# The down projection of a transformer block as seven block products instead of eight

## The chip, the cores and the metric

The kernel runs on one core of one Trainium2 chip. The metric is the device time of one execution in microseconds (us), lower being better. A difference under 0.2% (about 2.8 us here) can't be told from no change.

## The reference

One block of a hybrid model on a sequence of 1024 rows with 1024 features, in float32: normalisation and input projection, a sparse attention and a gated linear attention side by side, an output projection with residual, and a feed-forward part. Only the last part matters here:

```python
h = h + jnp.concatenate([o_nsa, o_gla], axis=-1) @ w_out[l]
u = causal_dwconv(rms_norm(h, ffn_norm[l]) @ w_up[l], conv_w[l], conv_b[l])
gate, up = jnp.split(u, 2, axis=-1)
h = h + (jax.nn.silu(gate) * up) @ w_down[l]
```

The product in the last line is the down product: activations of 1024 rows by 2816 channels times weights of 2816 channels by 1024 features. Its result is added to `h` and leaves the chip.

## The kernel before, in words

Every matrix product is made of float32r factors in two parts. ScalarE copies a float32 tile into a "high" part (`hi_of`, L57), VectorE subtracts that from the source and keeps the rest as the "low" part (`lo_of`, L60); together that is a `split` (L89). TensorE then makes three matmuls for each pair of tiles, high by high, high by low and low by high. Each is 128x128 by 128x512 and adds into one PSUM bank of 128x512.

The kernel is recorded with a tile framework that has a scheduler of its own: it puts the instructions of each engine in an order, and each engine then works strictly in that order. SyncE (SP) issues nearly all loads, one after another; a load whose buffer is still in use holds up all loads behind it. Buffers come from pools on two ends of the memory; a pool that opens where an older one was closed has to wait for that one's last readers, tile by tile.

The work runs in stages: input projection and attention (to about 600 us), output projection (to about 730 us), up product (to 1157 us), down product (to the end).

The up product runs over 22 channel blocks `j`. Its blocks from the fourth on are already made as one level of Strassen's scheme: `up` (L834) makes seven products `prod` of 12 matmuls, in the order B11, T2, T1, T3, B21, B22, T4 of its right-hand factors (`fac`, split tiles that stay in memory for the whole stage). The `gated` step (L771) applies the convolution and the gate with ScalarE and VectorE and writes 128 channels by 1024 rows to a scratch tensor `act_d` in DRAM.

The down product (L869 to L912) runs over two halves of the features (`hf`) and, in each, over eight row tiles of 128 rows. `act_load` brings the activations of one row tile back in three loads and splits them with all 22 channel blocks in one tile; the weights `wD` of a half are loaded and split once, and stay. Each row tile takes 22 x 3 = 66 matmuls into one bank; VectorE adds `h` (L911) and ScalarE's queue sends the tile out (L912). That is 2 x 8 x 66 = 1056 matmuls. A row tile needs all 22 channel blocks, so its last loads wait for the last block of the up product.

Of the kernel before, what the change touches and what calls it, by code (L numbers as in the profile page):

```python
# [34 lines left out]
def body(tc, I, out, tap=lambda name, ap: None):  # L35
# [51 lines left out]
    act_d = [dr.tile([NT, 128, 8, 128], F, name=f"act_d{i}") for i in range(3)]  # L87
# [567 lines left out]
    k2 = pool(es, "k2", 18, side="right")  # L655
# [6 lines left out]
    for f in ("B11", "B21", "B22", "B12"):  # L662
        facp[f] = pool(sF, "fac" + f, side="right")
        fac[f] = tuple(facp[f].tile([128, 4, 512], R, name=f"f{f}{p}", tag=p) for p in "hl")
    h = {(t, hf): k2_tile(name="h") for t in range(NT) for hf in range(2)}
    facp["T3"] = pool(sF, "facT3", side="right")
# [63 lines left out]
    with ExitStack() as sp:  # L730
        fc = pool(sp, "fc")
        cw = fc.tile([128, 2 * NJ, 3], F, name="cw")
        cb = fc.tile([128, 2 * NJ], F, name="cb")
        SY.dma_start(cw, I["cw"])
        SY.dma_start(cb, I["cb"])
        for f in ("T3", "T1", "T2"):
            if f not in facp:
                facp[f] = pool(sF, "fac" + f, side="right")
            fac[f] = tuple(facp[f].tile([128, 4, 512], R, name=f"f{f}{p}", tag=p) for p in "hl")
        wr = pool(sp, "wr", 3)  # L740
        wsp = pool(sp, "wsp", 1)
        ttp = pool(sp, "ttp", 4)
# [28 lines left out]
        def gated(j, us):  # L771
            ys = []
            for b in range(2):
# [9 lines left out]
            SY.dma_start(act_d[j // 8][:, :, j % 8].rearrange("t p q -> p t q"),  # L783
                         ys[1].rearrange("p (t q) -> p t q", q=128))
# [81 lines left out]
    sF.close()  # L866


    with ExitStack() as sp:  # L869
        pad = pool(sp, "pad")  # L870
        pad.tile([128, 192], F, name="pad")
        dB = pool(sp, "dB", 32, side="right")
        dA = pool(sp, "dA", 20, side="right")
        ar = pool(sp, "ar", 2)
        ah_a = pool(sp, "ah_a", 4)
        ah_p = pool(sp, "ah_p", 10)
        pd = pool(sp, "pd", 4, PSUM)

        def act_load(t):
            got = []  # L880
            for i in range(3):
                n = min(8, NJ - 8 * i)
                raw = ar.tile([128, 8, 128], F, name="araw")[:, :n]
                SY.dma_start(raw, act_d[i][t, :, :n])
                x, y = ((ah_p if i else ah_a).tile([128, 8, 128], R, name=m, tag="ahl")[:, :n] for m in ("ah", "al"))
                split(x, y, raw, V)
                got += [(x[:, j], y[:, j]) for j in range(n)]
            return got

        for hf in range(2):  # L890
            sl = slice(hf * 512, hf * 512 + 512)
            dws = {}
            for ts in ([0, 1], [2], [3], [4], [5], [6], [7]):
                acts = {t: act_load(t) for t in ts}
                ps = {t: pd.tile([128, 512], F, name="pd") for t in ts}
                for j in range(NJ):
                    if j not in dws:
                        raw = k2_tile(name="wdraw")
                        SY.dma_start(raw, I["wD"][j, :, sl])
                        dws[j] = tuple((dA if j < 10 else dB).tile([128, 512], R, name=n, tag="d") for n in ("dh", "dl"))  # L900
# [115 lines left out]
```

## Time and profile before

| | |
|---|---|
| median of 3 runs | 1418.25 us (1416.62 to 1418.8) |
| profiled execution | 1420.06 us, of which its span is 1418.3 us |
| granted TensorE clock, mean over the span | 0.983 of full speed |
| TensorE (PE) busy | 1349.2 us, 95% |
| VectorE (DVE) busy | 1003.6 us, 71% |
| ScalarE (ACT) busy | 688.3 us, 49% |
| GpSimd (POOL) busy | 334.6 us, 24%, nothing after the output projection |
| DMA | 174.19 MB, mean 123 GB/s |

PE is the row of matmuls and PEld that of the weight loads, which overlap them. A matmul row lasts 0.39 us, but one starts every 0.227 us, so that the distance of starts, not the row's length, is its price. The same holds on VectorE and ScalarE, whose successive instructions overlap by about 0.1 us. In square brackets at a row's end stands how long the engine was idle before it and what ended that.

### The profile page before, as it was taken

How to read it: one execution, taken by the hardware profiler on the slowest of the kernel's cores; microseconds unless marked ns; L12 is line 12 of the kernel's file. 1: busy time of each engine (PE TensorE's matmuls, PEld its weight loads, DVE VectorE, ACT ScalarE, POOL GpSimd, SP SyncE). 2: the span in 40 equal slices, each digit the busy share in tenths (PEclk: the TensorE clock that was granted, in tenths of full speed). 3: DMA queues.
4: the chain of work that ended last, by engine and by line, in shares of the span. 5: the costliest groups of instructions: out<-in, count | busy, mean ns of one | idle time of the engine just before them, and what ended most of it. 6: DMA issues, size and time to landing. Idle time of an engine off the chain costs nothing.

```text
span 1418.3 us, 19798 instructions
## 1 busy us (share of the span) xinstructions
PE 1349.2 (95%) x6750; PEld 1125.3 (79%) x6750; DVE 1003.6 (71%) x2433; ACT 688.3 (49%) x1390; POOL 334.6 (24%) x491
## 2 busy tenths in 40 slices
PE   6998989999999999999969999999999989999998
PEld 5876878887888887777858888888888867887887
DVE  7985856878787789843889888888788884325320
ACT  5332656777665677653544544444444462214210
POOL 5343655538444464425200000000000000000000
PEclk9999999999999999999989999999999998999999
DMA  8536673325221332116630222222222165437430
GB/s 306 179 126 231 186 239 111 110 70 161 85 93 57 102 103 79 38 53 195 194 127 15 89 76 88 70 79 89 90 89 76 58 215 182 163 134 245 159 126 23
DMA packets 92904, 174.19 MB, mean 123 GB/s; under 512 B 9970, under 2 KB 44675, under 8 KB 92803
## 3 DMA queue, kind: packets, MB, share of 16 engines
q1 hardware_dynamic: 66818, 108.95, 23.7%
q0 software_dynamic: 10368, 37.75, 8.8%
q10 hardware_dynamic: 15616, 26.22, 5.1%
q8 instruction: 53, 0.87, 0.3%
q14 instruction: 49, 0.39, 0.1%
HBM read 130.95 MB, written 41.94 MB: 122 GB/s over the span
## 4 chain that ended last, share of the span: by engine, by line
PE 78%; DVE 10%; DMA 4%; ACT 3%; issue 2%; POOL 2%; SPq 0%; ACTq 0%; DVEq 0%; POOLq 0%
PE pd L906 16%; PE O L466 4%; PE z L118 4%; PE z L120 4%; PE z L119 4%; PE S L448 4%; PE pt L459 3%; PE uX L764 3%; PE uX L766 3%; PE uX L765 3%; PE uZ L764 3%; PE uZ L766 3%; PE uZ L765 3%; PE uW L764 3%; PE uW L766 3%; PE uW L765 3%
## 5 line engine op out<-in xcount | busy, mean ns | idle before, releaser
L118 PE MATMUL z<-whi,xt 128*128 128x512 f32 (+1 forms) x384 | 143.1, 373 | 5.7 <-DVE vv L204 2.7
L906 PE MATMUL pd<-dh,ah 128*128 128x512 f32 x352 | 137.7, 394 | 7.4 <-ACT ah L57 4.7
L906 PE MATMUL pd<-dh,al 128*128 128x512 f32 x352 | 138.6, 394 | 4.7 <-DVE al L60 4.7
L119 PE MATMUL z<-wlo,xt 128*128 128x512 f32 (+1 forms) x384 | 141.1, 367 | 0.4 <-DMA w<-in_w_dram 0.4
L120 PE MATMUL z<-whi,xt 128*128 128x512 f32 (+1 forms) x384 | 140.6, 366 | 0.0
L906 PE MATMUL pd<-dl,ah 128*128 128x512 f32 x352 | 138.7, 394 | 0.5 <-DVE dl L60 0.5
L60 DVE TENSOR_TENSOR al<-araw,ah 128x1024 fp32r<-128x1024 f32 (+1 forms) x48 | 54.3, 1136 | 107.2 <-ACT ah L57 106.1
L60 DVE TENSOR_TENSOR PTl<-pt,PTh 128x512 fp32r<-128x512 f32 (+1 forms) x148 | 99.9, 684 | 32.8 <-ACT PTh L57 32.1
L57 ACT ACTIVATE ah<-araw 128x1024 fp32r<-128x1024 f32 (+1 forms) x48 | 47.2, 988 | 153.0 <-DMA araw<-act_d 87.4
L453 ACT ACTIVATE P<-P,m 128x640 f32<-128x640 f32 (+7 forms) x128 | 94.1, 736 | 53.4 <-DVE m L450 52.0
L57 ACT ACTIVATE PTh<-pt 128x512 fp32r<-128x512 f32 (+1 forms) x148 | 85.3, 592 | 52.0 <-PE pt L459 49.3
L527 POOL TENSOR_SCALAR P<-P,sc 128x640 f32<-128x640 f32 (+7 forms) x128 | 89.6, 710 | 83.5 <-DVE sc L473 54.6
L448 PE MATMUL S<-kst,qst 128*128 128x320 f32 (+5 forms) x384 | 99.9, 351 | 3.7 <-DVE m L450 3.3
L57 ACT ACTIVATE wuh<-wuraw 128x512 fp32r<-128x512 f32 x65 | 40.9, 633 | 113.3 <-PE uZ L765 73.0
L118 PEld LDWEIGHTS z<-whi,xt 128*128 128x128 f32 x384 | 74.1, 193 | 16.6 <-issue 5.1
L459 PE MATMUL pt<-ident,P 128*128 128x128 f32 x528 | 86.4, 274 | 0.8 <-DVE PTl L60 0.6
L906 PEld LDWEIGHTS pd<-dh,ah 128*128 128x128 f32 x352 | 67.1, 191 | 22.1 <-ACT ah L57 5.1
L119 PEld LDWEIGHTS z<-wlo,xt 128*128 128x128 f32 x384 | 74.2, 193 | 10.5 <-DVE wlo L60 0.8
L906 PEld LDWEIGHTS pd<-dh,al 128*128 128x128 f32 x352 | 67.1, 191 | 19.3 <-DVE al L60 5.2
L120 PEld LDWEIGHTS z<-whi,xt 128*128 128x128 f32 x384 | 74.2, 193 | 10.1
L906 PEld LDWEIGHTS pd<-dl,ah 128*128 128x128 f32 x352 | 66.9, 190 | 15.1 <-DVE dl L60 1.0
L459 PEld LDWEIGHTS pt<-ident,P 128*128 128x128 f32 x528 | 66.1, 141 | 15.9 <-issue 1.4
(455 smaller groups left out, 3684.1 us busy)
## 6 DMA issues: line engine op xcount, KB each, us to landing
xt<-x_d POOLq DMA_DIRECT2D x48, 512.0 KB, 3.8
wuraw<-in_wU_dram SPq DMA_DIRECT2D x42, 512.0 KB, 3.4
araw<-act_d SPq DMA_DIRECT2D x32, 512.0 KB, 3.4
act_d<-y SPq DMA_DIRECT2D x22, 512.0 KB, 3.4
wdraw<-in_wD_dram SPq DMA_DIRECT2D x44, 256.0 KB, 5.3
x_d<-xt ACTq DMA_DIRECT2D x16, 512.0 KB, 4.7
xt<-mix_d POOLq DMA_DIRECT2D x16, 512.0 KB, 4.4
araw<-act_d SPq DMA_DIRECT2D x16, 384.0 KB, 3.0
```

Of the source, the lines that this page charges most:

```text
L57: A.activation(dst, src, AF.Copy, scale=scale)
L60: (eng or V).tensor_sub(dst, src, hi.bitcast(F))
L118: T.matmul(ps, x[:, 0], wh, start=(k == 0), stop=False)
L119: T.matmul(ps, x[:, 0], wl, start=False, stop=False)
L120: T.matmul(ps, x[:, 1], wh, start=False, stop=(k == NK - 1))
L448: T.matmul(ps[:, :e - c], qst[:, h], kcols(i, c, e), start=(i == 0), stop=(i == 1))
L453: A.activation(Pt, Pt, AF.Exp, bias=m, scale=-1.0, accum_out=sc)
L459: T.transpose(tp[:n, h], get(h), ident)
L764: T.matmul(ps, wh[:, k], bh[:, k], start=(k == 0 and not add), stop=False, skip_group_check=True)
L765: T.matmul(ps, wh[:, k], bl[:, k], start=False, stop=False, skip_group_check=True)
L766: T.matmul(ps, wl[:, k], bh[:, k], start=False, stop=(k == 3 and last), skip_group_check=True)
L906: T.matmul(ps[t], l, r, start=(j == 0 and n == 0), stop=(j == NJ - 1 and n == 2))
```

## The change

The down product becomes one level of Strassen's scheme (in Winograd's form) over halves of the rows, the features and the channels. Block products are numbered P1 to P7 and run in the order P1, P2, P6, P5, P7, P3, P4. Each runs over 11 channel blocks `j` (`NH`), and each of these 77 steps takes a left factor of 512 rows and a right factor of 512 features and makes 4 row tiles x 3 = 12 matmuls into a set of four PSUM banks. Two sets, `a` and `b`, take turns; P3 adds to the banks of P5, and P4 to those of P7.

Per channel block a tile `g[j]` of four 128x512 slots is kept: first weight and activation of P1, then two more blocks for P2, which P6 turns in place into the sums that P6, P5, P3 and P4 use (lines 917 to 920 of the new file). What isn't kept is loaded again into a ring of six buffers `dv` (pool `stg`) of two slots. The split parts lie in a ring of six steps (pools `ring0` to `ring2`). The scratch tensor is now one tensor per channel block with whole rows. The constants `cw` and `cb` are loaded earlier, and some pools change places.

```diff
-    act_d = [dr.tile([NT, 128, 8, 128], F, name=f"act_d{i}") for i in range(3)]
+    act_d = [dr.tile([128, S], F, name=f"act_d{j}") for j in range(NJ)]
...
+    cw = late.tile([128, 2 * NJ, 3], F, name="cw")
+    cb = late.tile([128, 2 * NJ], F, name="cb")
+    SY.dma_start(cw, I["cw"])
+    SY.dma_start(cb, I["cb"])
...
-    for f in ("B11", "B21", "B22", "B12"):
+    for f in ("B12", "B22", "B21", "T3", "B11"):
...
-        cw = fc.tile([128, 2 * NJ, 3], F, name="cw")
-        cb = fc.tile([128, 2 * NJ], F, name="cb")
-        SY.dma_start(cw, I["cw"])
-        SY.dma_start(cb, I["cb"])
-        for f in ("T3", "T1", "T2"):
+        for f in ("T3", "T2", "T1"):
...
-            SY.dma_start(act_d[j // 8][:, :, j % 8].rearrange("t p q -> p t q"),
-                         ys[1].rearrange("p (t q) -> p t q", q=128))
+            SY.dma_start(act_d[j], ys[1])
...
-        for hf in range(2):
-            for ts in ([0, 1], [2], [3], [4], [5], [6], [7]):
-                acts = {t: act_load(t) for t in ts}
...
-                        for n, (l, r) in enumerate(((a, w), (a, wl), (al, w))):
-                            T.matmul(ps[t], l, r, start=(j == 0 and n == 0), stop=(j == NJ - 1 and n == 2))
...
+        NH = NJ // 2
+        stg = pool(sp, "stg", 6, side="right")
+        hxp = pool(sp, "hxp", 6, side="right")
...
+        rings = [pool(sp, f"ring{i}", side="right") for i in range(3)]
...
+        def a_in(dst, m, k, j):
+            SY.dma_start(dst, act_d[j + NH * k][:, 512 * m:512 * m + 512])
+
+        def b_in(dst, k, n, j):
+            SY.dma_start(dst, I["wD"][j + NH * k, :, 512 * n:512 * n + 512])
+
+        def staged(a, b, j):
+            v = stg.tile([128, 2, 512], F, name="dv")
+            a_in(v[:, 0], *a, j)
+            b_in(v[:, 1], *b, j)
+            return v
...
+        def p1_in(j):
+            return G[j][:, 0:2], 1
+
+        def p2_in(j):
+            a_in(G[j][:, 2], 1, 0, j)
+            b_in(G[j][:, 3], 1, 1, j)
+            return staged((0, 1), (1, 0), j), 0
+
+        def p6_in(j):
+            w, g = staged((1, 1), (0, 1), j), G[j]
+            V.tensor_tensor(g[:, 2], g[:, 2], w[:, 0], op=OP.add)
+            V.tensor_tensor(g[:, 0], w[:, 1], g[:, 0], op=OP.subtract)
+            V.tensor_tensor(g[:, 1], g[:, 2], g[:, 1], op=OP.subtract)
+            V.tensor_tensor(g[:, 3], g[:, 3], g[:, 0], op=OP.subtract)
+            return g[:, 1::2], 0
+
+        def p5_in(j):
+            return G[j][:, 0::2], 1
+
+        def p7_in(j):
+            v, w = staged((0, 0), (1, 1), j), staged((1, 0), (0, 1), j)
+            V.tensor_tensor(v, v, w, op=OP.subtract)
+            return v, 0
+
+        def p3_in(j):
+            v = staged((0, 1), (1, 1), j)
+            V.tensor_tensor(v[:, 0], v[:, 0], G[j][:, 1], op=OP.subtract)
+            return v, 0
...
+        def factors(get, j):
+            src, s = get(j)
+            i = step[0] % 6
+            step[0] += 1
+            fh, fl = (rings[i // 2].tile([128, 2, 512], R, name=f"d{n}{i}", tag=f"d{n}{i}") for n in "hl")
+            split(fh, fl, src, V)
+            return (fh[:, s], fl[:, s]), (fh[:, 1 - s], fl[:, 1 - s])
...
+        def product(get, ps, add, mid, end, outer=NH):
+            for j in range(outer):
+                ab = factors(get, j)
+                for t in range(4):
+                    mul(ps, t, ab, j, add)
+                if j == 4 and mid:
+                    for t in range(4):
+                        mid(t)
+            rest = [(j, factors(get, j)) for j in range(outer, NH)]
+            for t in range(4):
+                for j, ab in rest:
+                    mul(ps, t, ab, j, add)
+                end(t)
...
+        product(p1_in, pa, False, None, lambda t: A.activation(u2[t], pa[t], AF.Copy))
+        product(p2_in, pb, False, rest_of(0, 0), result(pb, 0, 0, hx))
+        product(p6_in, pa6, False, None, plus(pa6, u2))
+        product(p5_in, pb, False, mid5, plus(pb, u4))
+        product(p7_in, pa, False, None, result(pa, 1, 1, u4))
+        product(p3_in, pb, True, rest_of(0, 1), result(pb, 0, 1, hx))
+        product(p4_in, pa, True, rest_of(1, 0), result(pa, 1, 0, hx), 5)
```

On TensorE the place is the seam from the up product (`uW`) to the down product. Before, `pd` is the bank of one row tile, `d` and `a` the split weights and activations (`h` high, `l` low):

```order
L766 MATMUL uW_12641<-fT4h_9882,wul_12750 128x512
L906 MATMUL pd_12849<-dh_12853,ah_12815 128x512
L906 MATMUL pd_12849<-dl_12854,ah_12815 128x512
L906 MATMUL pd_12849<-dh_12853,al_12816 128x512
L906 MATMUL pd_12849<-dh_12865,ah_12815 128x512
L906 MATMUL pd_12849<-dl_12866,ah_12815 128x512
```

And now, where `pda0` to `pda3` are the four banks of set `a`, and `dh0`, `dl0` hold both factors of step 0:

```order
L766 MATMUL uW_12657<-fT4h_9898,wul_12766 128x512
L953 MATMUL pda0_12890<-dh0_12894 128x512
L953 MATMUL pda0_12890<-dl0_12895,dh0_12894 128x512
L953 MATMUL pda0_12890<-dh0_12894,dl0_12895 128x512
L953 MATMUL pda1_12891<-dh0_12894 128x512
L953 MATMUL pda1_12891<-dl0_12895,dh0_12894 128x512
L953 MATMUL pda1_12891<-dh0_12894,dl0_12895 128x512
```

One split now feeds 12 matmuls in four banks; the rows L953 number 924, the rows L906 were 1056.

On SyncE's queue the place is the end of the up product. Before, `act_d` is written in three tensors, and the loads of the first row tiles stand right behind the third last write:

```order
L783 DMA act_d2_70<-y1_12317 128x8x128
L750 DMA wuraw_12627<-in_wU_dram 128x1024
L783 DMA act_d2_70<-y1_12468 128x8x128
L884 DMA araw_12813<-act_d0_68 128x1024
L884 DMA araw_12819<-act_d1_69 128x1024
L899 DMA wdraw_12851<-in_wD_dram 128x512
```

And now, a few rows behind the same write (number 20 of 22 in the up product's order), where `g3`, `g4`, `g5` are the tiles kept per channel block:

```order
L893 DMA g3_12831<-in_wD_dram 128x512
L890 DMA g3_12831<-act_d3_71 128x512
L893 DMA g4_12832<-in_wD_dram 128x512
L890 DMA g4_12832<-act_d4_72 128x512
L890 DMA g3_12831<-act_d3_71 128x512
L783 DMA act_d20_88<-y1_12635 128x1024
L893 DMA g5_12826<-in_wD_dram 128x512
L890 DMA g5_12826<-act_d5_73 128x512
```

`g3` and `g4` lie where the factor T3 of the up product lay, `g5` and `g6` where B21 lay, `g7` and `g8` where B22, `g9` and `g10` where T4. From the first of these rows to the first load for P6 (into `dv_13333`) the queue has 67 transfers, of 256 KB each but for two writes of 512 KB.

On VectorE the place is the seam from P2 to P6. Before, VectorE had splits of activations and one addition per row tile in the middle of the down product:

```order
L60 TENSOR_TENSOR al_13314<-araw_13311,ah_13313 128x1024
L60 TENSOR_TENSOR al_13308<-araw_13305,ah_13307 128x1024
L60 TENSOR_TENSOR al_13320<-araw_13317,ah_13319 128x768
L911 TENSOR_TENSOR o_13212<-pd_13143,hx_13210 128x512
L60 TENSOR_TENSOR al_13404<-araw_13401,ah_13403 128x1024
```

And now, where `dl3_13306` belongs to the last step of P2 and the sums of lines 917 to 920 to P6:

```order
L60 TENSOR_TENSOR dl2_13285<-dv_13281,dh2_13284 128x1024
L917 TENSOR_TENSOR g0_12845<-g0_12845,dv_13333 128x512
L60 TENSOR_TENSOR dl3_13306<-dv_13302,dh3_13305 128x1024
L918 TENSOR_TENSOR g0_12845<-dv_13333,g0_12845 128x512
L919 TENSOR_TENSOR g0_12845<-g0_12845 128x512
L917 TENSOR_TENSOR g1_12849<-g1_12849,dv_13356 128x512
L918 TENSOR_TENSOR g1_12849<-dv_13356,g1_12849 128x512
L920 TENSOR_TENSOR g0_12845<-g0_12845 128x512
L917 TENSOR_TENSOR g2_12853<-g2_12853,dv_13379 128x512
```

From the sum of `g0` in the second of these rows to the split of P6's sixth step (`dl3_13456`) VectorE has 53 instructions: 40 sums and 4 additions out of PSUM of 128x512, and 7 splits and 2 differences for P7 of 128x1024.

## Rows read from the trace of the kernel before

**Rows 1.** The page: span, busy time by engine, shares of the chain that ended last

```profile
span 1418.3 us, 19798 instructions
PE 1349.2 (95%) x6750; PEld 1125.3 (79%) x6750; DVE 1003.6 (71%) x2433; ACT 688.3 (49%) x1390; POOL 334.6 (24%) x491
PE 78%; DVE 10%; DMA 4%; ACT 3%; issue 2%; POOL 2%; SPq 0%; ACTq 0%; DVEq 0%; POOLq 0%
```

**Rows 2.** Windows: start:end length, busy per engine (count), granted clock, DMA share, GB/s

```profile
1170.00:1200.00 30.00, 27.05 (x109) 22.17 (x110) 12.44 (x13) 8.90 (x9) 0.00 (x0) 0.87 0.52 166
1230.00:1260.00 30.00, 30.00 (x134) 24.86 (x133) 8.28 (x9) 5.94 (x6) 0.00 (x0) 1.00 0.40 135
```

**Rows 3.** Timeline of PE: start, length, engine, line, operation, output<-inputs

```profile
1157.13 0.39 PE L906 MATMUL pd<-dh,ah 128*128 128x512 f32 x1
...
1239.64 0.39 PE L906 MATMUL pd<-dh,ah 128*128 128x512 f32 x1
...
1242.36 0.39 PE L906 MATMUL pd<-dh,ah 128*128 128x512 f32 x1
...
1414.21 0.39 PE L906 MATMUL pd<-dh,al 128*128 128x512 f32 x1
```

**Rows 4.** Groups by shape from 1130 us on: busy, mean ns, idle before, releasers

```profile
L906 PE MATMUL pd<-dl,ah 128*128 128x512 f32 x352 | 138.7, 394 | 0.5 <-DVE dl L60 0.5
L906 PE MATMUL pd<-dh,al 128*128 128x512 f32 x352 | 138.6, 394 | 4.7 <-DVE al L60 4.7
L906 PE MATMUL pd<-dh,ah 128*128 128x512 f32 x352 | 137.7, 394 | 7.4 <-ACT ah L57 4.7 <-ACT dh L57 2.7
```

**Rows 5.** Timeline of PE: the two long waits of the down product

```profile
1167.40 0.50 PE L906 MATMUL pd<-dh,ah 128*128 128x512 f32 x1 [4.67 <-ACT ah L57]
...
1172.95 0.79 PE L906 MATMUL pd<-dh,al 128*128 128x512 f32 x1 [4.67 <-DVE al L60]
```

**Rows 6.** Windows at half clock and under the densest loads

```profile
1173.00:1178.00 5.00, 5.00 (x12) 3.94 (x13) 0.32 (x1) 0.84 (x1) 0.00 (x0) 0.50 0.58 202
1294.00:1298.00 4.00, 4.00 (x12) 3.10 (x11) 3.46 (x6) 3.25 (x6) 0.00 (x0) 0.57 0.96 352
1302.00:1308.00 6.00, 6.00 (x28) 4.97 (x27) 3.89 (x6) 4.05 (x7) 0.00 (x0) 1.00 0.99 332
```

**Rows 7.** Groups by shape from 1130 us on: splits and the last addition

```profile
L60 DVE TENSOR_TENSOR al<-araw,ah 128x1024 fp32r<-128x1024 f32 x32 | 39.0, 1225 | 61.4 <-ACT ah L57 60.3 <-PE pd L906 1.1
L57 ACT ACTIVATE ah<-araw 128x1024 fp32r<-128x1024 f32 x32 | 33.7, 1059 | 94.0 <-DMA araw<-act_d 67.7 <-PE pd L906 24.0 <-DVE al L60 1.3
L911 DVE TENSOR_TENSOR o<-pd,hx 128x512 f32<-128x512 f32 x16 | 11.1, 691 | 54.7 <-PE pd L906 51.8 <-DMA hx<-h_d 2.9
```

**Rows 8.** Timeline of DVE: starts that follow each other without a wait

```profile
734.40 0.69 DVE L807 TENSOR_TENSOR tt<-fB12h,fB11h 128x512 f32<-128x512 f32 x1
735.00 0.68 DVE L60 TENSOR_TENSOR fB22l<-hg,fB22h 128x512 fp32r<-128x512 f32 x1
...
1138.84 1.22 DVE L60 TENSOR_TENSOR al<-araw,ah 128x1024 fp32r<-128x1024 f32 x1 [1.21 <-ACT ah L57]
1139.98 1.28 DVE L778 SCALAR_TENSOR_TENSOR y<-u,cw,y 128x1023 f32<-128x1023 f32 x1
```

**Rows 9.** Loads: SP's issues of 22 weight tiles, landing of the 44, of `hx`

```profile
1287.41 18.44 SPq L899 DMA_DIRECT2D wdraw<-in_wD_dram  x22
...
DMA to landing us min/median/max: 2.6/5.3/7.4
...
hx<-h_d SPq DMA_DIRECT2D x16, 256.0 KB, 3.7
```

**Rows 10.** Timeline of SP and PE where the up product begins

```profile
712.21 0.38 SPq L734 DMA_DIRECT2D cw<-in_cw_dram  x1
...
714.90 0.42 SPq L749 DMA_DIRECT2D wuraw<-in_wU_dram  x1
...
727.54 1.97 PE L719 MATMUL hT<-ident,hn 128*128 128x128 f32 x8 [7.97 <-ACT hn L716]
```

More of the change, by code (lines that the diff above doesn't have):

```diff
@@ L866, in body @@
     sF.close()
+    sK.close()
     with ExitStack() as sp:
[L870 to L888, printed above, removed]
@@ new lines, in body @@
+        u2 = [up_.tile([128, 512], F, name=f"u2{t}") for t in range(4)]
+        u4 = [up_.tile([128, 512], F, name=f"u4{t}") for t in range(4)]
+        pd = pool(sp, "pd", 1, PSUM)
+        step = [0]
+        def a_in(dst, m, k, j):
[7 more added lines that the diff above has]
+            return v
@@ new lines, in p5_in, with p4_in @@
+        def p5_in(j):
[8 more added lines that the diff above has]
+            return v, 0
+        def p4_in(j):
+            v = staged((1, 1), (1, 0), j)
+            V.tensor_tensor(v[:, 1], v[:, 1], G[j][:, 3], op=OP.subtract)
+            return v, 0
@@ new lines, in factors, with mul @@
+        def factors(get, j):
[5 more added lines that the diff above has]
+            return (fh[:, s], fl[:, s]), (fh[:, 1 - s], fl[:, 1 - s])
+        def mul(ps, t, ab, j, add):
+            (ah, al), (bh, bl) = ab
+            ts = slice(t * 128, t * 128 + 128)
+            for n, (l, r) in enumerate(((ah, bh), (ah, bl), (al, bh))):
+                T.matmul(ps[t], l[:, ts], r, start=(j == 0 and n == 0 and not add), stop=(j == NH - 1 and n == 2),
+                         skip_group_check=True)
@@ new lines, in bank_set, with rest_of, mid, result @@
+        def bank_set(c):
+            return [pd.tile([128, 512], F, name=f"pd{c}{t}") for t in range(4)]
+        hx = {}
+        def rest_of(m, n):
+            def mid(t):
+                hx[t] = hxp.tile([128, 512], F, name="hx")
+                rows(hx[t], t + 4 * m, n)
+                V.tensor_tensor(hx[t], hx[t], u2[t], op=OP.add)
+            return mid
+        def result(ps, m, n, acc):
+            def end(t):
+                V.tensor_tensor(acc[t], ps[t], acc[t], op=OP.add)
+                put(acc[t], t + 4 * m, n)
+            return end
@@ new lines, in plus, with mid5 @@
+        def plus(ps, acc):
+            return lambda t: V.tensor_tensor(acc[t], ps[t], acc[t], op=OP.add)
+        def mid5(t):
+            rows(u4[t], t + 4, 1)
+            V.tensor_tensor(u4[t], u4[t], u2[t], op=OP.add)
+        for j in range(NH):
+            b_in(G[j][:, 0], 0, 0, j)
+            a_in(G[j][:, 1], 0, 0, j)
+        pa = bank_set("a")
+        product(p1_in, pa, False, None, lambda t: A.activation(u2[t], pa[t], AF.Copy))
+        pb = bank_set("b")
+        product(p2_in, pb, False, rest_of(0, 0), result(pb, 0, 0, hx))
```

43 lines of the change are left out of this document (20 added, 23 removed).

## The prediction

> **What bounds the kernel now.** I read the page first: TensorE is busy for 95% of the span and makes up 78% of the chain of waits [rows 1], so time comes from fewer matmuls or from TensorE's waits. Then the windows: in the middle of the down product TensorE is never idle while VectorE has 8 of 30 us of work, but where the stage begins the clock falls and TensorE idles [rows 2]. The timeline gives the price of a matmul: 12 starts in 1242.36 - 1239.64 = 2.72 us, 0.2267 us each; the first of the stage starts at 1157.13, the last at 1414.21 [rows 3]. So 1056 matmuls take 1055 x 0.2267 = 239.2 of the 257.1 us. Of the other 17.9 us, 12.6 are waits before line 906 [rows 4], most of them the two of 4.67 us at the start, for the activations of the first row tiles [rows 5], which need the up product's last block. The remaining 5.3 us went at half clock: behind those waits 12 matmuls ran in 5 us [rows 6], where 22 do at full clock.
>
> **What the change removes.** 1056 - 924 = 132 matmuls, x 0.2267 = 29.9 us, all of them on TensorE's path. The wait at the seam goes: P1 uses channel blocks 0 to 10 alone, and the order has its first three splits in front of the up product's last evictions, so TensorE goes on without a pause. If nothing were late, the last matmul would start at 1157.1 + 923 x 0.2267 = 1366.3, and with the tail behind it, 1418.3 - 1414.2 = 4.1 us as now (one addition and one store), the span would be 1370.4. What is late next is the question.
>
> **What it adds on VectorE.** 77 splits of 128x1024, 44 sums of 128x512 for P6, 11 differences of 1024 for P7, 22 of 512 for P3 and P4, 36 additions of results and rows of `h`. Successive starts are 0.60 us apart for 512 columns and 1.14 for 1024 [rows 8]: 88 x 1.14 + 102 x 0.60 = 161.5 us against 209 of matmuls, so on average there is room. By product a step costs 1.14 in P1, P2 and P5, 1.74 in P3 and P4 and 2.28 in P7, under the 2.72 of its matmuls, but 1.14 + 4 x 0.60 = 3.54 in P6. Where P6 has no lead, TensorE waits. ScalarE has 77 copies of 1.06 us [rows 7], 82 us, hidden beside the rest; P1's four evictions to ScalarE and the swap of bank sets cost nothing, since a set is needed again one product (29.9 us) later. P6's lead comes from the loads.
>
> **The loads before P6.** `g3` lies where the up factor T3 lay. T3 is the fourth of seven products of 12 matmuls in the last block, so its memory is free 3 x 2.72 = 8.2 us before that block ends, at 1148.9, and with the issue the load goes out at about 1149.4. From there SP's queue is a dense stream: to P6's first load 67 transfers, two of them double, 69 units of 256 KB. The first lands 2.6 us after its issue, the shortest of the weight loads [rows 9]. How fast a unit follows the last, bounded: 262144 B at 352 GB/s, the densest window, is 0.745 us; 22 loads of this size were issued in 18.44 us, 0.84 each [rows 6, 9]. I take 0.79, from the window with the DMA engines busy for 99%, 332 GB/s [rows 6]. So the 69th lands at 1152.0 + 68 x 0.79 = 1205.7.
>
> From that landing VectorE has 53 instructions up to the low part of P6's sixth step: 44 x 0.60 + 9 x 1.14 = 36.7 us, done at 1242.4. TensorE, undelayed, gets there after 27 steps (22 of P1 and P2, 5 of P6): 1157.1 + 27 x 2.72 = 1230.5, plus the four matmuls of the step that the order puts ahead and that need only the high part, 0.9: 1231.4. The difference, **11.0 us**, is lost, spread over P6's first six steps. At 0.745 the landing is 3.1 us earlier and the loss 7.9; at 0.84 it is 3.4 later and the loss 14.4. Behind that step VectorE has only splits of 1.14 and a few differences, so P5 finds it ahead again.
>
> Before P6 the same stream must feed P2: the load for its seventh step (`dv_13218`) is unit 60, landing at 1198.6; with copy and split about 2.3 us more, 1200.9, against TensorE's need at 1157.1 + 17 x 2.72 = 1203.3. Nothing lost, with 2.4 us in hand; at 0.84 us the hand is empty and about 0.5 us is lost.
>
> A rule of the Trainium skill speaks against this: "DMA: Bandwidth & Descriptors", section Bandwidth, advises batches of 1 MiB or more for 75% of the peak, and its section on the anatomy of one DMA has a fixed 2.0 us on each, which makes 2.6 us for 256 KB, an estimate from that page. The shortest landing, 2.6, agrees for a single load; the 22 in 18.44 us [rows 9] show that it isn't paid in turn, since several are in flight. Were it paid in turn, the 69 units would take 179 us; that end is the fourth rival.
>
> **The clock.** Behind the 9.3 us of waits [rows 5] TensorE's clock was granted at 0.5, its lower level of 1.2 GHz [rows 6]; the whole stage lost 5.3 us to that beside 12.6 of waits. The new waits are of the same sum, but each is shorter with matmuls between. Bounds 0 and 5.3; I take **3**.
>
> **The load ring.** In P3 and P4 each split frees the buffer whose two loads a later difference waits for, and VectorE keeps its order. For two steps: the issue 0.37, the landing, one difference 0.60, one split 1.22 [rows 7]. With a landing of 2.6 that is 4.8, with the 3.7 of `hx`, which follows another load [rows 9], 5.9, against 5.44 on TensorE. So 0 to 0.23 us a step, 0 to 5 over 22 steps; the lead of up to five steps hides it, except that P4 finishes bank by bank and needs its last six splits together. I take **1**. P7 loads 4 x 0.79 = 3.16 a step, 0.44 more than TensorE takes, 4.8 us in all, hidden by what is fetched during P5, which loads nothing for 29.9 us; bounds 0 and 4.8, taken 0.
>
> **Elsewhere.** The order outside the down product is as before but for a few rows where the up product begins. There TensorE waits 7.97 us for `hn`, held up behind weight splits [rows 10]. Without `cw` and `cb` at 712.2 the first weight loads can go out up to 2.7 us earlier (they went at 714.9 [rows 10]); against that a split of 0.6 us or two now stands before the square root's last rows. Bounds -2.7 and +1.2, taken 0. Writing `act_d` in whole rows is off the path.
>
> **The sum.** 1370.4 + 11.0 + 3 + 1 = 1385.4, of the profiled execution's span; that execution took 1420.06, 1.8 more than its span, while the median of the runs is 1418.25, the span's own number. So the forecast is **1385 us**, 2.3% faster. Its own range goes from 1370.4 + 7.9 - 2.7 = 1376 to 1370.4 + 14.4 + 5.3 + 3 = 1393.
>
> **Rivals.**
> 1. *P6 is nearly covered.* The stream runs at 352 GB/s and the clock holds: 1370.4 + 7.9 = 1378. For it: the window that reached that rate [rows 6]. Against it: the rate held for 4 us, and the waits at the seam did lower the clock. 13%.
> 2. *The load ring binds.* If landings take 3.7 us or more under load, P3 and P4 lose their 5 us, P7 its 4.8, with P6 as forecast: 1385.4 + 9 = about 1395. For it: the median landing of the weight loads was 5.3 [rows 9]. Against it: that was with many queued, in the ring two are. 18%.
> 3. *The change doesn't do what it says* would mean that matmuls come back; the order has 924 of them, so I give it no chance of its own.
> 4. *Slower than before: the loads become the bound of the whole stage.* From `g3` to the last load there are about 194 units. With the rest of P4 and the tail behind the last landing (0.6 + 1.1 + 1.2 + 57 x 0.227 + 4.1 = 20 us) the end passes 1418.3 when a unit takes (1418.3 - 20 - 1152.0)/193 = 1.28 us, that is under 205 GB/s. The windows of the stage show 135 to 166 GB/s [rows 2], which at first sight speaks for it; but there the DMA engines were busy for only 0.40 to 0.52, so the demand was the limit. The page's rule on small transfers, weighed above, would lead here too. At 1.3 us a unit the time is 1152.0 + 193 x 1.3 + 20 = 1423; I give 1425. 7%.
>
> The forecast keeps 62%. Faster by over 0.2% holds in it and in rivals 1 and 2, and in hardly any of 4: 0.91; within 0.2%, a rate just at the limit in 4: 0.02; slower: 0.07. A change under 0.2% can't be told from none here. The range: 1374 (below rival 1, if the start of the up product gains as well) to 1402 (above rival 2), leaving out rival 4 and half of the ends.
>
> **What would show it.** PE rows of the new line 953: 924, a start every 0.2267 us. At the seam no wait. In P6, some 65 to 90 us after the stage begins, waits of TensorE for low parts (`dl`) of 10 to 14 us in all, ended by VectorE, with VectorE busy without a pause and the first sum of `g0` at about 1206, waiting for its load. No wait of size in P1, P2, P5. A half-clock stretch in or behind P6. The forecast is wrong if TensorE waits in P3, P4 or P7 for more than 3 us in all (rival 2), if the sum of `g0` comes after 1212 (the stream is slower than the bounds), or if VectorE's successive starts are longer than 0.60 and 1.14 under the denser loads.

## The result and the profile after

The changed kernel takes 1381.67 us (median of four executions, 1379.50 to 1387.36), against 1417.78 for the kernel before: a ratio of 0.9746, 95% interval 0.973 to 0.9761. The forecast was 1385 us. The profiled execution is the slowest of the four, 1387.36 us with a span of 1385.6; the prediction's sum, made for a span, was 1385.4. A second set of four executions of the same file (the control below) gave 1384.03 us, 1381.65 to 1386.70. The page after, in the lines of [rows 1]:

```profile
span 1385.6 us, 19733 instructions
PE 1319.1 (95%) x6618; PEld 1099.7 (79%) x6618; DVE 1077.0 (78%) x2519; ACT 698.3 (50%) x1379; POOL 334.9 (24%) x491
PE 68%; DVE 14%; DMA 10%; ACT 3%; issue 3%; POOL 2%; SPq 1%; ACTq 0%; DVEq 0%; POOLq 0%
```

TensorE has 132 matmuls less and is still busy for 95%; VectorE and DMA have a larger share of the chain than before: something new is late now and then. The timeline of TensorE at the seam, and its last matmul, answer to [rows 3]:

```profile
1156.33 0.39 PE L766 MATMUL uW<-fT4h,wul 128*128 128x512 f32 x1
1156.55 0.39 PE L953 MATMUL pda<-dh 128*128 128x512 f32 x1
...
1381.28 0.39 PE L953 MATMUL pda<-dh,dl 128*128 128x512 f32 x1
```

The stage goes on without a pause and lasts 1381.28 - 1156.55 = 224.7 us from first start to last. 924 matmuls need 923 x 0.2267 = 209.2, so 15.5 us are lost, as against 17.9 before on 1056. The groups of TensorE from 1130 us on (busy, mean ns, idle before, releaser; compare [rows 4]):

```profile
L953 PE MATMUL pda<-dl,dh 128*128 128x512 f32 x176 | 70.2, 401 | 10.0 <-DVE dl L60 10.0
L953 PE MATMUL pda<-dh,dl 128*128 128x512 f32 x176 | 69.6, 398 | 0.0
L953 PE MATMUL pda<-dh 128*128 128x512 f32 x176 | 65.5, 398 | 0.0
L953 PE MATMUL pdb<-dh,dl 128*128 128x512 f32 x132 | 51.4, 389 | 0.0
```

All waits are for low parts, and all in products of bank set `a`; the rows of set `b` (P2, P5, P3) have none. The timeline says where (in brackets the wait before the matmul):

```profile
1224.29 0.50 PE L953 MATMUL pda<-dl,dh 128*128 128x512 f32 x1 [1.39 <-DVE dl L60]
...
1231.98 0.50 PE L953 MATMUL pda<-dl,dh 128*128 128x512 f32 x1 [1.93 <-DVE dl L60]
...
1237.80 0.50 PE L953 MATMUL pda<-dl,dh 128*128 128x512 f32 x1 [2.76 <-DVE dl L60]
...
1360.26 0.50 PE L953 MATMUL pda<-dl,dh 128*128 128x512 f32 x1 [1.57 <-DVE dl L60]
1362.36 0.79 PE L953 MATMUL pda<-dl,dh 128*128 128x512 f32 x1 [1.13 <-DVE dl L60]
1365.23 0.79 PE L953 MATMUL pda<-dl,dh 128*128 128x512 f32 x1 [1.22 <-DVE dl L60]
```

Three waits stand in P6, 6.1 us, and three in P4, 3.9 us. The other 5.5 us went mostly at the lower level of TensorE's clock, 1.2 GHz, behind or among them (windows: length, busy by engine, granted clock, DMA share, GB/s; the first two show the dense loads up to P6 and into its first steps):

```profile
1156.00:1187.00 31.00, 31.00 (x139) 25.66 (x138) 22.10 (x21) 17.29 (x19) 0.00 (x0) 1.00 1.04 383
1187.00:1217.00 30.00, 30.00 (x134) 24.86 (x133) 23.68 (x32) 10.80 (x11) 0.00 (x0) 1.00 0.97 347
1237.00:1243.00 6.00, 5.21 (x16) 4.14 (x17) 6.00 (x8) 1.68 (x2) 0.00 (x0) 0.72 0.60 214
1359.00:1370.00 11.00, 7.39 (x21) 5.11 (x22) 8.87 (x10) 4.84 (x5) 0.00 (x0) 0.69 0.27 85
```

And VectorE where P2 passes to P6, with the end of its chain:

```profile
1188.60 1.22 DVE L60 TENSOR_TENSOR dl<-dv,dh 128x1024 fp32r<-128x1024 f32 x1
1195.88 5.17 DVE L60 TENSOR_TENSOR dl<-dv,dh 128x1024 fp32r<-128x1024 f32 x4 [6.06 <-ACT dh L57]
1200.96 0.68 DVE L917 TENSOR_TENSOR g<-g,dv 128x512 f32<-128x512 f32 x1
1201.56 1.22 DVE L60 TENSOR_TENSOR dl<-dv,dh 128x1024 fp32r<-128x1024 f32 x1
...
1236.50 3.51 DVE L60 TENSOR_TENSOR dl<-g,dh 128x1024 fp32r<-128x1024 f32 x3
```

From the sum of `g0` to the end of the first split in the last row is 1236.50 + 1.2 - 1200.96 = 36.7 us, the prediction's number for the 53 instructions; TensorE goes on at 1237.80. But the chain began at 1200.96, where the prediction had 1205.7, and not with a wait for its load: that load was issued at 1195.33 and landed 5.3 us later, at 1200.6, while VectorE was in the last of four splits of P2. From there to 1237.7 VectorE has no wait at all, for a load or for another engine.

### The profile page after: what moved, and what is told of

Read it like the earlier page. It is cut to its first block, busy times and chain, and to the rows that moved or that the text cites. A ratio compares the mean times of both kernels' runs of the same rounds, so it can differ in the third digit from the quotient of the medians.

```text
span 1385.6 us, 19733 instructions
## 1 busy us (share of the span) xinstructions
PE 1319.1 (95%) x6618; PEld 1099.7 (79%) x6618; DVE 1077.0 (78%) x2519; ACT 698.3 (50%) x1379; POOL 334.9 (24%) x491
## 4 chain that ended last, share of the span: by engine, by line
PE 68%; DVE 14%; DMA 10%; ACT 3%; issue 3%; POOL 2%; SPq 1%; ACTq 0%; DVEq 0%; POOLq 0%
PE z L118 4%; PE z L119 4%; PE z L120 4%; PE O L466 4%; DMA dv<-in_wD_dram 4%; PE S L448 4%; PE pt L459 3%; PE uX L765 3%; PE uX L764 3%; PE uX L766 3%; PE uZ L765 3%; PE uW L765 3%; PE uW L764 3%; PE uZ L766 3%; PE uW L766 3%; PE uZ L764 3%
## 5 line engine op out<-in xcount | busy, mean ns | idle before, releaser
L57 ACT ACTIVATE dh<-dv 128x1024 fp32r<-128x1024 f32 x44 | 46.0, 1059 | 76.3 <-PE pda L953 19.8
L953 PE MATMUL pda<-dl,dh 128*128 128x512 f32 x176 | 70.2, 401 | 10.0 <-DVE dl L60 10.0
L57 ACT ACTIVATE wuh<-ws 128x512 fp32r<-128x512 f32 x76 | 47.8, 629 | 52.5 <-PE uW L765 41.7
L777 ACT ACTIVATE y<-u,cb,cw 128x1024 f32<-128x1024 f32 x44 | 54.7, 1243 | 37.6 <-DVE u L853 17.4
L448 PEld LDWEIGHTS S<-kst,qst 128*128 128x128 f32 x384 | 62.3, 190 | 13.2 <-DVE m L450 7.6
L953 PE MATMUL pda<-dh,dl 128*128 128x512 f32 x176 | 69.6, 398 | 0.0
L778 DVE SCALAR_TENSOR_TENSOR y<-u,cw,y 128x1023 f32<-128x1023 f32 x44 | 56.4, 1283 | 16.8 <-ACT y L777 16.8
L60 DVE TENSOR_TENSOR dl<-dv,dh 128x1024 fp32r<-128x1024 f32 x44 | 53.4, 1221 | 17.0 <-ACT dh L57 15.3
```

The source lines that it names most:

```text
L57: A.activation(dst, src, AF.Copy, scale=scale)
L60: (eng or V).tensor_sub(dst, src, hi.bitcast(F))
L448: T.matmul(ps[:, :e - c], qst[:, h], kcols(i, c, e), start=(i == 0), stop=(i == 1))
L953: T.matmul(ps[t], l[:, ts], r, start=(j == 0 and n == 0 and not add), stop=(j == NH - 1 and n == 2), skip_group_check=True)
```

## The experiments

All are compared with the control, the changed kernel unaltered. Its waits are 4.5 us in P6 and 3.0 in P4, its stage lasts 221.5 us. The stage began at 1159.05 there, 2.5 us later than in the first trace: what lies before the stage varies by a few us from one execution to another, so that times between the experiments are read with the length of the stage. Between these two traces of the same kernel the waits differ by 1.6 us in P6 and by 0.9 in P4; smaller differences between single traces mean nothing.

> The changed kernel unaltered, as the measure for the others on the same chip. Theory A (VectorE's chain into P6) and its rivals expect the same of it: 1381 us (1379 to 1385), 10 us of waits before line 953, of which about 6 in P6 and 4 in the last product; if the waits come out otherwise by more than 1 us from one execution to the next, differences below that size in the other kernels mean nothing.

**1. Half of P6's sums on GpSimd.**

```diff
-            V.tensor_tensor(g[:, 0], w[:, 1], g[:, 0], op=OP.subtract)
+            P.tensor_tensor(g[:, 0], w[:, 1], g[:, 0], op=OP.subtract)
...
-            V.tensor_tensor(g[:, 3], g[:, 3], g[:, 0], op=OP.subtract)
+            P.tensor_tensor(g[:, 3], g[:, 3], g[:, 0], op=OP.subtract)
```

> The two sums of weights per step of P6 (lines 918 and 920) go from VectorE to GpSimd, which has nothing else to do there. Theory A (TensorE's waits in P6 are the chain of 53 VectorE instructions, 36.7 us): about 20 of the 40 sums leave the chain, 24 x 0.60 + 9 x 1.14 = 24.7 us, done at 1225.7 against a need of 1231; GpSimd needs 12 x 1.35 = 16 us for its part, beside it. P6's 6.1 us of waits go, and the half clock behind them (3.4 us at half, 1.7 lost): 1381.7 - 7.8 = 1374. Rival C (the waits are those for the landing of P6's own loads, and VectorE's name on them is only the last link): P6's waits stay at 4 us or more, 1380 to 1382. Rival D (GpSimd's sums lengthen VectorE's, since both read and write the same memory): VectorE's successive starts rise above 0.60, the waits fall by less than half.

Measured: 1395.63 us, ratio to before 0.9839 (0.9821 to 0.9856), 11.6 us more than the control. The timelines of VectorE and of GpSimd in P6:

```profile
1206.32 3.48 DVE L917 TENSOR_TENSOR g<-g,dv 128x512 f32<-128x512 f32 x2
1209.72 3.48 DVE L919 TENSOR_TENSOR g<-g 128x512 f32<-128x512 f32 x2
1213.12 1.78 DVE L917 TENSOR_TENSOR g<-g,dv 128x512 f32<-128x512 f32 x1
```

```profile
1209.20 1.74 POOL L920 TENSOR_TENSOR g<-g 128x512 f32<-128x512 f32 x1
1210.90 1.74 POOL L918 TENSOR_TENSOR g<-dv,g 128x512 f32<-128x512 f32 x1
1212.61 1.74 POOL L920 TENSOR_TENSOR g<-g 128x512 f32<-128x512 f32 x1
```

Two sums take VectorE 1209.72 - 1206.32 = 3.40 us, 1.70 each instead of 0.60, and GpSimd starts one every 1.70 too (16 additions of this size earlier in the first trace took it 1.29 us at the median). So VectorE with half of the sums takes longer than with all; P6's waits grow to 11.7 us, and the clock falls behind them (window from 1217 to 1247 us):

```profile
1217.00:1247.00 30.00, 18.29 (x53) 13.61 (x52) 30.00 (x25) 6.07 (x6) 24.20 (x14) 0.73 0.42 141
```

Rival D held, and beyond what it said: the waits grew. The page "SBUF — State Buffer" of the Trainium skill, section "SBUF: two separate sides", has the two engines share a pair of ports that one instruction locks as a whole, when VectorE has two inputs in that memory; the trace agrees that neither keeps its pace, though strict turns would make 0.60 + 1.29 = 1.89 and it shows 1.70.

**2. Half of the sums left out.** The same two lines are taken out, so that half of P6's sums are missing from the result.

> The two sums of weights of each step of P6 (lines 918 and 920) are left out altogether, so that half of the sums of P6, P5, P3 and P4 are missing from the product; loads, splits and matmuls are as in the changed kernel. It is the run on GpSimd again without a second engine on the same memory. Theory A (P6's waits are VectorE's count of instructions): the chain from the sum of g0 to the split of P6's sixth step loses about 20 sums, 20 x 0.60 = 12 us, and is done some 6 us before TensorE needs it: P6's waits (4.5 in the control, 6.1 in the first trace) go to 0, with them the half clock there (1.8 us lost); 1384.0 - 6.3 to 7.9 = 1376 to 1378. VectorE's sums stay at 0.60 from start to start, against 1.70 in the run on GpSimd. Rival C (the loads): 4 us or more of P6's waits stay, 1382 or more.

Measured: 1377.21 us, ratio 0.9702 (0.9688 to 0.9717). P6 has no wait at all; 2.5 us stay, all in P4. Here too the window from 1217 to 1247 us answers, now at full clock and with TensorE never idle:

```profile
1217.00:1247.00 30.00, 30.00 (x134) 24.83 (x133) 26.23 (x30) 11.83 (x12) 0.00 (x0) 1.00 0.74 245
```

P6's waits are VectorE's count of instructions, as theory A has it. The loads are issued as before, but those of weights for P6 have no reader here, so that this run alone can't clear them; the first trace does, where VectorE has no wait inside the chain. The first experiment failed by contention, not by its idea.

**3. Eight more loads ahead of P6.**

```diff
+        dum = pool(sp, "dum")
...
+            if j == 0:
+                for i in range(8):
+                    b_in(dum.tile([128, 512], F, name=f"dum{i}"), 0, 0, i)
             w, g = staged((1, 1), (0, 1), j), G[j]
```

> Eight more loads of 256 KB, of weights that nothing uses, stand on SyncE's queue among P2's last loads and ahead of P6's first. With 0.69 us each they delay P6's first load by 5.5 us, about to where the prediction had it (1205.7). Theory A (landing, then a chain of 36.7 us): the sum of g0 starts at about 1206.5 on the axis of the first trace (49.9 after the stage's first matmul, against 44.4), the sixth step's low part is ready 5.5 us later (86.6 after the first matmul, against 81.1), and P6's waits with the clock lost among them grow by 5.5; 1384.0 + 5.5 = 1389.5. Theory B in its strong form (the ring of split parts alone sets the chain's start and the landing has room): the growth is under 2 us, 1386 or less.

Measured: 1389.70 us, ratio 0.9804 (0.9784 to 0.9824), 5.7 more than the control. The sum of `g0` now waits for its load, 49.3 us after the stage's first matmul (1156.14):

```profile
1205.40 0.69 DVE L921 TENSOR_TENSOR g<-g,dv 128x512 f32<-128x512 f32 x1 [1.06 <-DMA dv<-act_d]
```

TensorE's last wait for P6's chain ends at 1241.70, against an undelayed 1156.14 + 27 x 2.72 + 0.9 = 1230.5: 11.2 us late. By the same measure the first trace is 1237.80 - 1230.9 = 6.9 us late. With the landing where the prediction put it, the loss in P6 is the 11 us that it named. Of these 7.2 show as waits; most of the rest passed at the lower clock between them, as in the window from 1222 to 1226 us:

```profile
1222.00:1226.00 4.00, 3.82 (x10) 3.00 (x11) 4.00 (x8) 1.06 (x1) 0.00 (x0) 0.59 0.92 249
```

**4. Four of the ten row loads held back.**

```diff
+            P.tensor_copy(u4[t][:, :1], G[NH - 1][:, 0, :1])
             rows(u4[t], t + 4, 1)
```

> The four loads of rows of h for u4, which stand among P2's loads on SyncE's queue, are held back until P6's last sum, so that P2's and P6's loads come four units of about 0.69 us earlier. Theory A in the form predicted (the chain of 53 starts when P6's first load lands): the sum of g0 starts at 1198.2 instead of 1201.0 and P6's waits fall by 2.8, to 3.3 us. Theory B (the landing and the ring of split parts bind at the same time: VectorE keeps its order, and the second instruction after the sum of g0 is a split of P2 whose slot TensorE gives back after 15 or 16 steps, 1156.6 + 15 x 2.72 = 1197.4 at the earliest): the chain starts about 1 us earlier whatever the landing, P6's waits stay at 5.0.

Measured: 1389.70 us, ratio 0.9801 (0.9784 to 0.9818), 5.7 us more than the control. The sum of `g0` starts at 1198.36, where theory A had it, but VectorE stops again at its next instruction, a split of P2:

```profile
1198.36 0.69 DVE L917 TENSOR_TENSOR g<-g,dv 128x512 f32<-128x512 f32 x1 [0.40 <-DMA dv<-act_d]
1199.45 1.23 DVE L60 TENSOR_TENSOR dl<-dv,dh 128x1024 fp32r<-128x1024 f32 x1 [0.40 <-ACT dh L57]
```

Up to the sixth split P6's waits are 5.0 us, as theory B said. The chain starts 41.0 us after the stage's first matmul instead of 44.4 in the first trace, but reaches the sixth split only at 78.8 instead of 79.9: two splits of P2 instead of one stand in it now, which follow TensorE through the ring of six split steps, one more sum (1.1 and 0.6 us), and a wait of 0.4. An earlier landing alone gains little; what stands on VectorE between the landing and the sixth split counts as much.

The way of holding the loads back brought a wait of its own. SyncE's queue waits for the one-column copies on GpSimd, of which the first takes 8.52 us; P7's loads stand behind the four held rows, and VectorE, in its order, behind P7's loads:

```profile
1234.11 8.88 POOL L992 COPY u<-g 128x1 f32<-128x1 f32 x4 [540.12 <-DVE g L918]
1242.65 1.74 SPq L902 DMA_DIRECT2D u<-h_d  x4
1249.47 1.23 DVE L928 TENSOR_TENSOR dv<-dv 128x1024 f32<-128x1024 f32 x1 [6.88 <-DMA dv<-in_wD_dram]
```

The splits behind that difference come late, and TensorE waits 1.1 us more in P6's last steps, which alternate with P5's first, and 0.2 in P5. In its profiled execution the stage (224.4 us) is 2.9 longer than the control's; why three other executions took another 1.6 to 3.4 us was not settled. Both `g0` rows that waited for their load also give the price of a unit: 12 units more moved it from 41.0 to 49.3 us after the stage's start, 0.69 us each.

**5. The last product by steps.**

```diff
-        product(p4_in, pa, True, rest_of(1, 0), result(pa, 1, 0, hx), 5)
+        product(p4_in, pa, True, rest_of(1, 0), result(pa, 1, 0, hx), 11)
```

> The last product runs all its 11 steps over four banks, instead of 5 steps and then bank by bank over the last six, so that it no longer needs its last six splits at once. Theory H (P4's waits, 3 to 3.9 us, come from the loop of loads into the ring of six: 5.54 us for two steps in the trace of the control against TensorE's 5.44, so that there is no lead left when the last six splits are wanted): the waits in P4 go to under 0.5 us, the half clock behind them shrinks; the tail grows, since four banks are added and stored at once, by up to 1.5 us: 1384.0 - 3 to 4 + 0.5 to 1.5 = 1380 to 1382. Rival I (the waits are ScalarE's and SyncE's, held up behind the stores of P3): they stay whatever the order of P4's matmuls, 1384 to 1386.

Measured: 1379.60 us, ratio 0.9719 (0.9698 to 0.9739). P4 has no wait left, the stage is 5.2 us shorter than the control's (216.3), and the tail did not grow: 4.3 us behind the last matmul's start, as in the control. It was the need for six splits at once that turned a loop without lead into waits. That loop, in the control's VectorE:

```profile
1337.08 0.69 DVE L938 TENSOR_TENSOR dv<-dv,g 128x512 f32<-128x512 f32 x1 [1.36 <-DMA dv<-in_wD_dram]
...
1342.60 0.69 DVE L938 TENSOR_TENSOR dv<-dv,g 128x512 f32<-128x512 f32 x1 [1.46 <-DMA dv<-in_wD_dram]
...
1348.16 0.69 DVE L938 TENSOR_TENSOR dv<-dv,g 128x512 f32<-128x512 f32 x1 [1.58 <-DMA dv<-in_wD_dram]
...
1358.72 0.69 DVE L938 TENSOR_TENSOR dv<-dv,g 128x512 f32<-128x512 f32 x1 [2.36 <-DMA dv<-in_wD_dram]
```

Two steps take 5.54 us (1337.08 to 1342.60 to 1348.16), against 5.44 on TensorE.

**6. The stores on GpSimd's queue**, first all of them, then all but the last product's. In the control ScalarE stands 8 us before a copy for P4, because a store of P3 ahead of it waits for VectorE:

```profile
1352.04 1.06 ACT L57 ACTIVATE dh<-dv 128x1024 fp32r<-128x1024 f32 x1 [7.99 <-DVE hx L984]
```

```diff
-            A.dma_start(out[t * 128:(t + 1) * 128, hf * 512:hf * 512 + 512], src)
+            P.dma_start(out[t * 128:(t + 1) * 128, hf * 512:hf * 512 + 512], src)
```

> The stores of results go out through GpSimd's queue instead of ScalarE's. In the control ScalarE stands 7.99 and 2.60 us before its copies for P4, held up behind the stores of P3's banks. Rival I (that is what makes P4 late): ScalarE's two waits go, and P4's waits of 3 to 3.9 us fall below 1 us; 1384.0 - 3 to 5 = 1379 to 1381. Theory H (the loop of loads): ScalarE's waits go, but VectorE still waits for the loads before line 938, about 15 us in all, and P4's waits stay within 1 us of the control's; 1383 to 1385. Rival D (GpSimd's work slows VectorE): only descriptors are made there, 16 of them, so no more than 1 us.

> Stores through GpSimd's queue for all results but the last product's, whose four stay on ScalarE's queue. In the run with all stores on GpSimd's queue P4's waits fell from 3.0 to 0.4 us, but the span ended 9.5 us after the last addition's start, against 3.9 in the control. Rival I (ScalarE and its stores are what makes P4 late) with that tail taken away: P4's waits under 1 us, the tail again 4 us, 1384.0 - 3 to 4 = 1380 to 1381. If the fall of P4's waits there was chance (they were 3.0 and 3.9 in two executions of the same kernel): P4's waits come back at 3 us, 1383 to 1385.

Measured: 1389.27 us (ratio 0.9788, 0.9767 to 0.9809) with all stores moved, 1383.13 (0.9756, 0.974 to 0.9772) with all but the last four. With all moved P4's waits are 0.4 us, but the end is a trap: the last store is issued at 1377.34, and the span ends only at 1385.9, 8.6 us later, where ScalarE's queue has the whole tail done in 4.3 us. It is not the transfer, which lands 2.3 us after its issue (2.0 from ScalarE's queue in the second kernel). GpSimd's closing instruction, a DRAIN that starts with that store, takes 7.8 us:

```profile
L1109 POOLq DRAIN  x3: 40/93/7822, 1377.3 to 1385.6; - x3
```

In the second kernel no DRAIN of GpSimd at the end takes over 0.1 us and the tail is 4.1 us again; P4's waits are 1.7 us, between the two theories. ScalarE's stop behind VectorE is gone in both kernels, and they differ only in stores that come after P4's waits, so that 0.4 and 1.7 are the spread of one case, against 3.0 and 3.9 with the stop. The stop thus makes a part of P4's waits; how large a part, these runs leave open. The second kernel's median is within the control's spread: no gain shown.

**7. Eight ordinary products in the same staging**, 1056 matmuls, no sums over blocks.

```diff
+        def block(m, n, k):
+            return lambda j: (staged((m, k), (k, n), j), 0)
...
+        for i, (m, n) in enumerate(((0, 0), (1, 0), (1, 1), (0, 1))):
+            ps = bank_set("ab"[i % 2])
+            product(block(m, n, 0), ps, False, None, lambda t: None)
+            product(block(m, n, 1), ps, True, rest_h(m, n), result(ps, m, n, hx), 5 if i == 3 else NH)
```

> Same staging, bank sets, scratch layout and rings, but eight ordinary block products (1056 matmuls) and no sums over blocks: each result is two products of 11 steps into one set of banks. It parts the gain into the staging by channel block and the seven products. Theory A: no wait at the seam, none inside, no half clock: 1156.6 + 1055 x 0.2267 + 4.0 = 1399.8, so 1400 (1398 to 1403); of the 36 us gained, 18 come from the staging alone and 18 from the seven products, whose 29.9 us of matmuls bring 12 us of new waits and lost clock with them. Rival E (the old waits were the loads' and come back in whatever order the channels run): 1406 or more with waits at the seam. Rival F (Strassen gives its full 29.9): 1411.

Measured: 1407.60 us (1404.79 to 1409.80), ratio 0.9922 (0.9901 to 0.9943). There is one wait, 3.5 us at the seam, not for a load but for a copy on ScalarE behind the up product's last `gated` step, and then none in 1056 matmuls:

```profile
1157.87 2.07 PE L922 MATMUL pda<-dh 128*128 128x512 f32 x4 [3.54 <-ACT dh L57]
```

In the chain of waits four pieces are the whole stage, the last three of them 264 x 0.2267:

```profile
1157.87 61.72 PE pda L922 x264
1219.59 59.84 PE pdb L922 x264
1279.43 59.84 PE pda L922 x264
1339.27 59.85 PE pdb L922 x264
```

So staging by channel block, with all else that the change does beside the seven products, is worth 1418.4 - 1407.6 = 10.8 us by itself, and seven products instead of eight 1407.6 - 1384.0 = 23.6 of their 29.9. The forecast for this run, 1400, was too low. In the profiled execution, with a span of 1403.0, the wait at the seam costs 3.5 and the clock behind it 1.9, as the first piece shows, while the up product ends 2.4 us earlier than in the first trace; why others took up to 5 us more was not settled.

**8. The rows in turn.** Four tiles hold the rows of three results one after another; the last result's rows lie in `u4`. The two tiles saved give 4 KB in each partition (not the 8 KB that the expectations name), the size of one more load buffer.

```diff
-        stg = pool(sp, "stg", 6, side="right")
-        hxp = pool(sp, "hxp", 6, side="right")
+        stg = pool(sp, "stg", 7, side="right")
+        hxp = pool(sp, "hxp", 4, side="right")
...
+                if kept:
+                    hx[t] = kept[t]
+                    A.activation(hx[t][:, :1], G[10][:, 0, :1], AF.Copy)
+                else:
+                    hx[t] = hxp.tile([128, 512], F, name="hx")
...
-            rows(u4[t], t + 4, 1)
+            h5[t] = hxp.tile([128, 512], F, name="hx")
+            rows(h5[t], t + 4, 1)
...
-        product(p4_in, pa, True, rest_of(1, 0), result(pa, 1, 0, hx), 5)
+        product(p4_in, pa, True, rest_of(1, 0, u4), result(pa, 1, 0, hx), 5)
```

> Four tiles for rows of h serve the results one after another, so that six of the ten row loads of 256 KB go out behind P6's loads instead of among P2's; the last result's rows lie in u4, held back by a one-column copy on ScalarE until P6's sums are done. The 8 KB that come free make a seventh buffer for the loads (stg 7). Theories A and B together (P6's chain starts when its first load has landed and the splits of P2 ahead of it have their slots): six units of 0.69 us earlier, the sum of g0 at about 1197 of the control's axis less its later start; P6's waits fall from 4.5-6.1 to about 2. Theory H: the seventh buffer gives the loop one step more of lead, P4's waits fall from 3-3.9 to about 1. Together with the half clock: 1384.0 - 4 to 8 = 1376 to 1380. Rival (as in the run with the rows held back by GpSimd): the row loads stand before P7's loads and bring new waits in P5; no gain, 1384 or more.

> The kernel with four tiles for rows in turn, but with six load buffers as in the changed kernel, so that the 8 KB stay unused: it parts the order of the row loads from the seventh buffer. If the order alone ended the waits: P6's waits stay under 2 us and P4's at 0, 1375 to 1377. If the seventh buffer did it in P4 (theory H): P6's waits stay under 2 us, but P4's come back at 2 to 3.5 us with the half clock behind them, 1378 to 1381.

Measured: 1375.18 us (1374.41 to 1376.38), ratio 0.9688 (0.9673 to 0.9702): faster than both kernels. The stage lasts 211.8 us, 2.6 above its matmuls. The groups of TensorE from 1130 us on, and the window of P6:

```profile
L953 PE MATMUL pda<-dl,dh 128*128 128x512 f32 x176 | 68.5, 391 | 1.1 <-DVE dl L60 1.0
...
L953 PE MATMUL pdb<-dh 128*128 128x512 f32 x132 | 50.0, 390 | 0.3 <-ACT dh L57 0.3
```

```profile
1217.00:1247.00 30.00, 28.62 (x122) 22.37 (x122) 30.00 (x38) 11.95 (x15) 0.00 (x0) 1.00 0.71 242
```

VectorE is as busy in P6 as ever, but its chain starts 40.5 us after the stage's first matmul (1198.17 - 1157.66; first trace 44.4) and its sixth split at 74.9 instead of 79.9. Of the 5.0 us, 3.9 come from the loads and 1.1 from the order that goes with them: P7's first two differences (1.14 us each) now stand behind that split, as its timeline shows, where in the first trace they stood ahead of it, and one more split of P2 stands in the chain:

```profile
1198.17 0.68 DVE L917 TENSOR_TENSOR g<-g,dv 128x512 f32<-128x512 f32 x1
...
1232.60 1.22 DVE L60 TENSOR_TENSOR dl<-g,dh 128x1024 fp32r<-128x1024 f32 x1
1234.34 2.35 DVE L928 TENSOR_TENSOR dv<-dv 128x1024 f32<-128x1024 f32 x2
```

The granted clock stays at 1.00 through the waits of 0.5 us. With six load buffers instead of seven the time is 1378.37 us (ratio 0.9717, 0.97 to 0.9735): P6's waits are the same, 1.4 us, P4's 0.8 instead of none, and the stage 213.5. Most of the gain is the order of the row loads; the seventh buffer takes the rest of P4's waits.

## Why the prediction was right, point by point

- **Matmuls and seam: right.** 924 rows, the first start 0.2 us behind the up product's last, no wait. The gain at the start of the up product, taken as 0, is not to be told from the spread of the stage's start (1156.1 to 1159.1).
- **P6, 11.0 us: the mechanism right, the size too large.** The three waits come to 6.1 us (control 4.5), ended by `dl`, and TensorE is 6.9 us late at the sixth step (control 6.7), below even the lower bound of 7.9. The step that failed is "How fast a unit follows the last": 0.745 to 0.84 us was taken from the densest rows of before [rows 6, 9]; why loads were slower there is not shown. Here the stream ran at 383 GB/s, 0.69 us a unit, and with its slower start 0.72 on average from the first landing (1148.59 + 3.1) to that of P6's first load (1200.6). So the landing came some 5 us early. The other half of the step, 36.7 us of VectorE, was right to a tenth, and experiment 3 shows that with the predicted landing the loss is the predicted one.
- **What the prediction left out there**: it took the chain as fixed at 53 instructions whenever its load lands. With an earlier landing splits of P2, bound to TensorE by the ring, move into it (experiment 4), so that rival 1's way down, a faster stream, ends at some 5 us of waits; in a kernel that does all its sums only another order of VectorE's work went below (experiment 8). The count of additions over the whole stage, 36, was a slip: the order has 40, which makes 163.9 us instead of 161.5 and changes nothing.
- **P2: right**, no wait; but VectorE stood 6.06 us there, and ScalarE 6.56 for a load, behind the row loads, so that the 2.4 us in hand were not much.
- **The clock, 3 us: too small**, 5.5 (control 4.8). The bound was taken from the same sum of waits before; but the waits now stand in two places and the clock falls behind both. Where a chain holds TensorE, clock lost between two of its waits makes the later wait shorter, so the two terms are not quite apart.
- **The load ring, 1 us: too small**, 3.9 (control 3.0), all in P4, and thereby past the 3 us that the prediction gave itself as the mark of rival 2. Its price per two steps, 4.8 to 5.9, holds the measured 5.54, and P3 and P7 lost nothing; what was mis-sized is the exception that it named, that P4 wants its last six splits together (experiment 5). Not foreseen was ScalarE's stop behind the stores, which makes a part of these waits (experiment 6).
- **The sum**: 11.0 + 3 + 1 = 15.0 predicted beyond the matmuls, 15.5 in the first trace and 12.3 in the control. The errors, 5 too much in P6, 2.5 too little for the clock and 3 for P4, cancel. That the forecast came nearer than its terms is luck.
- **The rule of the page "DMA: Bandwidth & Descriptors"** of the Trainium skill, weighed in the prediction, section Bandwidth: the trace doesn't bear it out for SyncE's loads that stand in a queue, where units of 256 KB ran at 383 GB/s; rival 4 was far off. The page's table there and its 2.0 us are for transfers issued from GpSimd, which the prediction doesn't say.

## What to carry to other kernels

When loads, a ring and an engine's fixed order meet at one place, work out the chain from each of them, since mending the latest gains only the distance to the next. Loads that are wanted late should not stand in the queue ahead of those that a chain starts from: moving six of them was worth about as much here as leaving half of VectorE's sums out. A product that finishes bank by bank asks for several steps of lead at its end; look whether the loop that feeds it has any.

## What the runs showed of the hardware

- VectorE's and GpSimd's additions of 128x512 beside each other both went at 1.70 us, instead of 0.60 and about 1.3: help from GpSimd cost 11.6 us. The first of four one-column copies on GpSimd beside a busy VectorE took 8.52 us and ended 0.05 us after VectorE's last instruction there, the other three 0.17 each (experiment 4; spans on GpSimd are rough).
- Loads of 256 KB issued by SyncE one after another held 383 GB/s over 31 us, with the DMA engines' share at 1.04; over the next 30 us, in whose second half SyncE issued them further apart, it was 347 and 0.97.
- A store of 256 KB from GpSimd's queue landed 2.3 us after its issue, but the closing DRAIN on GpSimd behind it took 7.8 us (experiment 6).
- The granted clock stayed at 1.00 through waits of 0.5 us (experiment 8) and through P4's waits of 2.3 and 0.2 (experiment 2, window below); behind the three waits in P6 of the first trace it stood at 1.2 GHz for 3.4 us, and behind the one of 3.5 at the seam of experiment 7 for as long.

```profile
1350.00:1371.00 21.00, 18.51 (x81) 14.51 (x80) 9.83 (x11) 4.14 (x5) 0.00 (x0) 1.00 0.22 80
```
